# Two transformer blocks on one core: an operand made in another's buffers, weight slabs split a product earlier, the residual input loaded in pieces, and a table spread later on another queue

## The chip, the core and the metric

The program runs on one NeuronCore of a Trainium2 chip. The core has five engines that take their instructions in program order: TensorE (PE) multiplies matrices, VectorE (DVE) and ScalarE (ACT) work elementwise, GpSimd (POOL) does some elementwise work and issues DMAs, and SyncE (SP) only issues DMAs. The engines meet through semaphores. Sixteen DMA engines move the data. The metric is device time of one execution in microseconds, the median of the runs of one kernel.

## The reference, cut to what matters

1,024 tokens of width 1,024 in float32 go through two blocks.

```python
def first_block(x, c, positions, ...):
    ...                       # mod: shift, scale and gate from silu(c) @ w_ada
    h = rms_norm(x, g_pre_mix) * (1.0 + scale1) + shift1
    ...                       # h @ w_in, short convolution and retention
    x = x + gate1 * rms_norm(mix @ w_out, g_post_mix)
    h = rms_norm(x, g_pre_mlp) * (1.0 + scale2) + shift2
    f = square(relu(h @ w_fc1)) @ w_fc2              # 1024 -> 4096 -> 1024
    return x + gate2 * rms_norm(f, g_post_mlp)

def second_block(x, positions, ...):
    z = rmsnorm(x, attn_norm_g) @ w_in
    y_a = dsa_sparse_attention(...)   # top 256 keys a query, bias table rel_bias
    y_b = mla_attention(...)          # latent attention
    x = x + (gate_a * (y_a @ w_branch_a) + gate_b * (y_b @ w_branch_b)) @ w_out
    x = x + square(relu(rmsnorm(x, mlp_norm_g) @ w_ff1)) @ w_ff2
    return rmsnorm(x, final_norm_g)
```

## The kernel before, in words

**Numbers.** Every float32 operand is parted into a rounded high part and the rest, its low part; a product is three matmuls into the same PSUM tile (high by high, high by low, low by high). For a weight slab ACT makes the high part `wh` from the raw slab `wr`, and DVE (in the attention stage POOL) the low part `wl`. Operands that TensorE streams lie in `u` tiles. A half H of the tokens is 512 wide, and activations of a half are eight pieces of 128x512 (256 KB), feature-major.

**Streams.** A `Stream` (`loads_ahead`, `split_ahead`, `next`) holds the order of slabs of one stage. Loads go out on SP in that order as soon as a buffer is promised; an entry can be held until an earlier entry has been split (`after`). SP is strictly in order: a load that waits for a buffer stops all behind it. The background scheduler `bg` steps generators between the products: that is how norms, residuals and stores get their places in the engines' programs.

**MLP of each block.** Both matrix products are done by a seven-product scheme on 2x2 parts. `up_first` makes the product P1 and the part A11 of the hidden layer for sixteen blocks q, two at a time: two half slabs from P1 for each, then two for A11. `up_rest` makes the rest. The hidden layer's four parts lie in HBM (`opd`). `down` runs seven passes P1, P2, P5, P6, P3, P7, P4, each of eight steps d, with a stream `fs` (`down_stream`) for the operands of the passes: A11 and A12 come through a ring of two buffers `t4`, tile name `t`; then the sums S1 = A21 + A22, S2 = S1 + A11 and S4 = S2 + A12 are chained in kept tiles `u` (`kept(d)`), by an SP load and DMAs on POOL's queue that add while they write; then S3 = A11 + A21 for P7 again comes through the ring of two: an SP load of A11, and an adding DMA of A21 on POOL's queue; then A22 for P4 through the ring.

**Residuals.** x of a half is kept in HBM (`xT`). In block 1's output projection the chain `chain_a` squares and adds on POOL (`sq_add`). In the down product `reload` fetches x of a half into a `u` tile with four 512 KB loads on POOL's queue among P7's adding DMAs, `chain_head` and `residual` add the MLP's output to it, and the new x goes back in one store of 2 MB after the norm. In block 2 `before_p7` loads token-major x (`xtokd`) for both halves on SP, 2 MB each; `first_out` and `second_out` add, `finish_last` ends the last half, token block by token block: add, square, reciprocal root, scale, store.

**z phase and attention.** `z_phase` makes the projections of block 2; its last ten products read slabs that POOL loads back (`wh<-slabd`, `wl<-slabd`), two buffers deep. Before them `bias_spread` has POOL write 4 MB (`biasd<-tab`). In `attention` a planner sets the order; SP loads bias slices (`u<-biasd`) and, in between, the last weights of the branches (`wr<-in_w_branch`).

All instructions go through one helper, so the profile gives line 183 for all; they are told apart by tiles.

Of the kernel before, what the change touches and what calls it, by code (L numbers as in the profile page):

```python
# [19 lines left out]
P = 128  # L20
# [323 lines left out]
class Stream:  # L344
# [7 lines left out]
    def __init__(self, m, split=3, slots=None):  # L352
        self.m, self.entries, self.split, self.slots = m, [], split, slots
        self.loads = self.splits = self.done = self.used = self.n_slots = 0
        self.parts, self.given, self.finished = {}, {}, set()
        self.rings = {}
        self.lo_engine = m.nc.vector

# [93 lines left out]
    def loads_ahead(self, n=None):  # L452
        while self.loads < len(self.entries) and (n is None or self.loads < n):
# [34 lines left out]
class Model:  # L488
# [202 lines left out]
    def residual(self, x, f, R, G, acc, engine=None, H=None):  # L691

        nc = self.nc
        for k in range(9):
            if k < 8:
                s = slice(k * T, k * T + T)
                t = self.t2()
                nc.vector.scalar_tensor_tensor(t, f[:, s], G[:, k:k + 1], R, op0=ALU.mult, op1=ALU.mult)
                nc.vector.tensor_add(x[:, s], x[:, s], t)
                if H is not None:  # L700
                    self.store_x(H, x, k)
            if k > 0:
                self.sq_add(acc, x[:, (k - 1) * T:k * T], k == 1, engine)
            yield "vector"
# [509 lines left out]
    def down_stream(self):  # L1214
# [50 lines left out]
        for d in range(8):  # L1265
            ringed(d, "A11", "A21")
# [270 lines left out]
    def block1(self):  # L1537
# [169 lines left out]
        def chain_a(f, acc):  # L1707
            yield from self.chain_head(xs[0], f, acc, G1, None, 0)
# [37 lines left out]
        def before_p7():  # L1746
            xs[0] = self.reload(0, 2)

        def after_p3():
            def chain():  # L1750
                yield from squares(0, 1)
                yield from self.chain_head(xs[0], self.outs[0], acc[0], G2, nc.vector)
# [3 lines left out]
                yield from self.norm_mod(xs[0], self.Rw, g_attn, None, *hs[0])  # L1756
                nc.gpsimd.dma_start(self.xT[:, 0], xs[0])
# [11 lines left out]
        self.down(False, {"P2": after_p2, "P3": after_p3, "P7": after_p7}, {"P7": before_p7, "P4": before_p4})  # L1769
# [9 lines left out]
        xs[0] = None  # L1779
        return xs, hs, self.outs[1], acc[1], G2  # L1780
# [10 lines left out]
    def chain_head(self, x, f, acc, G, engine=None, H=None):  # L1791
# [4 lines left out]
        yield from self.residual(x, f, R, G, acc2, engine, H)  # L1796
        self.Rw = self.r_tile()
# [23 lines left out]
    def bias_spread(self):  # L1821
# [4 lines left out]
        self.nc.gpsimd.dma_start(dst, src)  # L1826
# [446 lines left out]
    def z_phase(self, xs, hs, f, acc, G2):  # L2273
# [10 lines left out]
        def start():  # L2284
            yield from self.chain_head(xs[1], f, acc, G2, nc.vector)
            hs[1] = self.pair()
            yield from self.norm_mod(xs[1], self.Rw, g_attn, None, *hs[1])
            nc.gpsimd.dma_start(self.xT[:, 1], xs[1])
            xs[1] = None
# [59 lines left out]
        self.bias_spread()  # L2349
# [10 lines left out]
        ws.lo_engine = nc.vector  # L2360

# [15 lines left out]
    def attention(self):  # L2377
# [34 lines left out]
        self.branch_weights(starts[15])  # L2412
        self.plan.run()
        ws.lo_engine = self.nc.vector
# [556 lines left out]
    def block2(self):  # L2971
# [3 lines left out]
        xs, hs, xt = [self.reload(0), None], [None, None], [None, None]  # L2975
# [36 lines left out]
        gf = []  # L3012

        def before_p7():
            for H in range(2):
                xt[H] = load(H)

        def load(H):
            x = self.U()
            nc.sync.dma_start(x, self.xtokd[:, H])  # L3020
            return x
# [4 lines left out]
        def first_out():  # L3026
            f, x = self.outs[0], xt[0]
            for b in range(4):
                s = slice(b * D, b * D + D)
                (nc.vector, nc.gpsimd)[b % 2].tensor_add(x[:, s], x[:, s], f[:, s])  # L3030
                yield 2
            for b in range(4):
                s = slice(b * D, b * D + D)
                nc.scalar.activation(f[:, s], x[:, s], AF.Square, accum_out=ss[0][:, b:b + 1])
                yield
            gf.append(f[:, 0:D])
            src = self.a["final_norm_g_2"]
            nc.gpsimd.dma_start(gf[0], bass.AP(tensor=src.tensor, offset=src.offset, ap=[[0, P], [1, D]]))
            self.rsqrt(y[0], ss[0][:, 0:4], 4, 1.0 / D)
            yield 4  # L3040
            for b in range(4):
                s = slice(b * D, b * D + D)
                nc.vector.scalar_tensor_tensor(x[:, s], x[:, s], y[0][:, b:b + 1], gf[0], op0=ALU.mult, op1=ALU.mult)
                yield 1
                nc.sync.dma_start(self.a["out"][b * P:b * P + P], x[:, s])
                yield 1

        def after_p7():
            bg.add(second_out())

        def second_out():
            f, x = self.outs[1], xt[1]
            for b in range(4):
                c0, c1 = (slice(b * D + c * T, b * D + c * T + T) for c in range(2))
                nc.gpsimd.tensor_add(x[:, c1], x[:, c1], f[:, c1])
                nc.vector.tensor_add(x[:, c0], x[:, c0], f[:, c0])
                yield 1
                nc.scalar.activation(f[:, c1], x[:, c1], AF.Square, accum_out=ss[1][:, 2 * b + 1:2 * b + 2])
                yield 1
                nc.gpsimd.tensor_mul(x[:, c1], x[:, c1], gf[0][:, T:D])  # L3060

        self.down(True, {"P3": after_p3, "P7": after_p7}, {"P7": before_p7})
        bg.finish()
        self.finish_last(xt[1], self.last, ss[1], y[1], gf[0])
# [70 lines left out]
```

## Time and profile before

| | before |
|---|---|
| runs, us | 2756.8, 2753.07, 2748.65; median 2753.07 |
| profiled execution, us | 2745.33 |
| its span, us | 2743.6 |
| TensorE busy | 2610.7 us, 95% of the span |
| VectorE, ScalarE, GpSimd busy | 69%, 49%, 14% |
| mean granted TensorE clock | 0.983 of full |
| DMA | 454.86 MB, mean 166 GB/s |

The profiled execution is 1.7 us longer than its span and 7.7 us under the median of the three runs. A timeline row has the start, the duration, the engine (`SPq` is an issue on SP's queue), the operation, what it writes and reads, and in brackets how long the engine stood idle before it and what ended that. `xN` counts merged instructions.

### The profile page before, as it was taken

The page shows a single profiled execution, that of the slowest core. Times are in us where ns is not written, and L with a number is a line of the kernel's source. Part 1 is how long each engine was busy: PE and PEld are TensorE (multiplying, and loading weights), DVE is VectorE, ACT ScalarE, POOL GpSimd, SP SyncE. Part 2 cuts the span into 40 slices and gives each one's busy share as a digit, 9 for nine tenths or more (in the row PEclk, how much of TensorE's full clock was granted, in tenths as well). Part 3 has the DMA queues.
Part 4 walks back from the last instruction along what each step waited for, and adds up shares of the span by engine and source line. Part 5 has one row for each costly group of instructions (what it writes and reads, how often), then busy time and mean ns, then how long its engine had stood idle before and what let it go on. Part 6 is the DMA issues. An engine that isn't in the chain of part 4 may idle for free. (4 is left out here: it accounts for less than half of the span.)

```text
span 2743.6 us, 33563 instructions
## 1 busy us (share of the span) xinstructions
PE 2610.7 (95%) x12037; PEld 2086.5 (76%) x12052; DVE 1881.1 (69%) x3213; ACT 1331.3 (49%) x2192; POOL 391.8 (14%) x409
## 2 busy tenths in 40 slices
PE   5999999899999999999998999899999999999987
PEld 4777777677888888777876777777887788887866
DVE  6684575777665477877889688786567466646657
ACT  4552114465444343445675477784235454433333
POOL 5041111300000020100211411420000000002012
PEclk8999999999999999999999999999999999999999
DMA  6546536654445695845546401453454564459773
GB/s 206 177 139 209 177 119 204 208 192 140 150 133 199 201 271 144 246 110 144 142 147 199 131 14 51 140 167 116 139 170 146 179 238 141 152 188 279 188 207 131
DMA packets 364572, 454.86 MB, mean 166 GB/s; under 512 B 34533, under 2 KB 258708, under 8 KB 363380
## 3 DMA queue, kind: packets, MB, share of 16 engines
q1 hardware_dynamic: 322584, 300.58, 35.1%
q0 software_dynamic: 41488, 151.99, 19.5%
q8 instruction: 95, 1.56, 0.2%
q14 instruction: 73, 0.60, 0.1%
q10 hardware_dynamic: 332, 0.14, 0.0%
HBM read 359.60 MB, written 96.18 MB: 166 GB/s over the span
## 5 line engine op out<-in xcount | busy, mean ns | idle before, releaser
L183 PE MATMUL ps<-u,wh 128*128 128x512 f32 (+1 forms) x3568 | 1138.2, 400 | 27.5 <-DMA wh<-slabd 10.3
L183 PEld LDWEIGHTS ps<-u,wh 128*128 128x128 f32 (+1 forms) x3568 | 668.4, 189 | 196.1 <-ACT wh L183 11.8
L183 PE MATMUL ps<-u,wl 128*128 128x512 f32 (+1 forms) x1784 | 710.3, 398 | 6.7 <-DVE wl L183 6.5
L183 PE MATMUL pd<-u,wh 128*128 128x512 f32 x1600 | 522.8, 408 | 4.7 <-ACT u L183 2.4
L183 PEld LDWEIGHTS ps<-u,wl 128*128 128x128 f32 (+1 forms) x1784 | 336.8, 189 | 95.8 <-DVE wl L183 13.4
L183 PEld LDWEIGHTS pd<-u,wh 128*128 128x128 f32 x1600 | 298.9, 190 | 80.3 <-issue 5.8
L183 DVE TENSOR_TENSOR wl<-wr,wh 128x1024 fp32r<-128x1024 f32 (+3 forms) x209 | 223.8, 1077 | 180.5 <-ACT wh L183 176.8
L183 PE MATMUL pd<-u,wl 128*128 128x512 f32 x800 | 318.1, 398 | 0.0
L183 ACT ACTIVATE wh<-wr 128x1024 fp32r<-128x1024 f32 (+3 forms) x221 | 201.9, 920 | 167.4 <-PE pd L183 74.7
L183 ACT ACTIVATE t<-ps 128x512 f32<-128x512 f32 (+5 forms) x339 | 172.0, 521 | 192.9 <-PE ps L183 182.1
L183 DVE TENSOR_TENSOR t<-ps,t 128x384 fp32r<-128x384 f32 (+3 forms) x354 | 192.4, 563 | 90.6 <-PE ps L183 61.1
L183 ACT ACTIVATE t<-t 128x512 f32<-128x512 f32 (+2 forms) x261 | 163.1, 627 | 160.6 <-DVE t L183 89.1
L183 ACT ACTIVATE u<-t 128x512 fp32r<-128x512 f32 (+4 forms) x174 | 145.3, 839 | 184.9 <-DVE t L183 111.0
L183 DVE TENSOR_TENSOR u<-u 128x512 f32<-128x512 f32 (+3 forms) x144 | 143.3, 999 | 65.6 <-ACT u L183 62.6
L183 ACT ACTIVATE wh<-u 128x1024 fp32r<-128x1024 f32 x96 | 101.3, 1055 | 163.4 <-PE ps L183 117.3
L183 PEld LDWEIGHTS pd<-u,wl 128*128 128x128 f32 x800 | 151.7, 190 | 37.0
L183 DVE TENSOR_TENSOR wl<-u,wh 128x1024 fp32r<-128x1024 f32 x96 | 117.9, 1228 | 87.2 <-ACT wh L183 87.0
L183 PE MATMUL pd<-wh,u 128*128 128x512 f32 x512 | 166.4, 404 | 8.9 <-ACT u L183 7.4
L183 PE MATMUL ps<-wh,u 128*128 128x512 f32 (+1 forms) x576 | 173.7, 383 | 0.6 <-DVE u L183 0.6
L183 DVE TENSOR_TENSOR u<-t,u 128x512 fp32r<-128x512 f32 (+3 forms) x145 | 132.0, 927 | 56.6 <-ACT u L183 56.5
L183 ACT ACTIVATE u<-ps 128x512 f32<-128x512 f32 (+2 forms) x171 | 95.7, 575 | 119.4 <-PE ps L183 113.5
L183 ACT ACTIVATE u<-u,topk 128x768 bf16<-128x768 f32 (+8 forms) x157 | 135.0, 860 | 34.2 <-DVE topk L183 32.3
(193 smaller groups left out, 3407.2 us busy)
## 6 DMA issues: line engine op xcount, KB each, us to landing
wr<-in_w_fc SPq DMA_DIRECT2D x64, 512.0 KB, 4.6
opd<-t SPq DMA_DIRECT2D x128, 256.0 KB, 4.1
t<-opd SPq DMA_DIRECT2D x64, 512.0 KB, 4.4
wr<-in_w_ff SPq DMA_DIRECT2D x64, 512.0 KB, 4.5
wr<-in_w_in SPq DMA_DIRECT2D x56, 512.0 KB, 4.1
u<-opd POOLq DMA_DIRECT2D x48, 512.0 KB, 11.8
u<-in_w_ada POOLq DMA_DIRECT2D x32, 512.0 KB, 4.7
wr<-in_w_out SPq DMA_DIRECT2D x32, 512.0 KB, 3.9
```

What stands on the lines that cost most here:

```text
L183: return fn(*args, **kw)
```

## The change

It does seven things.

1. `up_first` asks for the split of the slabs two entries on after the first of the two A11 products.
2. `down_stream` makes S3 in the kept tiles of S4 (SP load of A21, adding DMA of A11), held until six entries before, instead of in the ring.
3. In block 1's down product and in the z phase x comes in eight pieces of 256 KB on SP into `t2` tiles (eight buffers), and the MLP's output tile takes the sum; xT is stored as four pieces of 512 KB as they are made.
4. `chain_a` adds its squares on DVE, not on POOL.
5. `bias_spread` issues on SP, behind the last slab products.
6. The stream's loads pause while the attention's plan runs.
7. In block 2 the two halves of `xtokd` come in eight pieces each, the first from the end of P3, the second behind the first half's stores in P4; all sixteen adds are on DVE, and the first half's output waits for P7's end.

```diff
@@ up_first
                 self.put_op("A11", q + i, f, 4)
+                if i == 0 and q < 14:
+                    ws.split_ahead(ws.used + 2)
@@ down_stream
-        def chained(d, *ops):
+        def chained(d, *ops, ahead=3):
...
-            s.entry(s.parts_of(lambda: kept(d), D), load, len(s.entries) - 3)
+            s.entry(s.parts_of(lambda: kept(d), D), load, len(s.entries) - ahead)
...
-            ringed(d, "A11", "A21")
+            chained(d, "A21", "A11", ahead=6)
@@ new: x_pieces, residual_in (chain_in calls them)
+        def load(k):
+            if k < 8:
+                xs[k] = self.t2()
+                self.nc.sync.dma_start(xs[k], self.xT[:, H, k * T:k * T + T])
...
+                nc.vector.scalar_tensor_tensor(f[:, s], f[:, s], G[:, k:k + 1], R, op0=ALU.mult, op1=ALU.mult)
+                nc.vector.tensor_add(f[:, s], f[:, s], xs.pop(k))
+                load(k + 2)
+                self.store_x(H, f, k)
+            if k > 0:
+                self.sq_add(acc, f[:, (k - 1) * T:k * T], k == 1, nc.vector)
@@ chain_a
-            yield from self.chain_head(xs[0], f, acc, G1, None, 0)
+            yield from self.chain_head(xs[0], f, acc, G1, nc.vector, 0)
@@ block 1, down product
-        def before_p7():
-            xs[0] = self.reload(0, 2)
...
-                yield from self.chain_head(xs[0], self.outs[0], acc[0], G2, nc.vector)
+                yield from self.chain_in(self.outs[0], acc[0], G2, 0)
...
-                nc.gpsimd.dma_start(self.xT[:, 0], xs[0])
...
-            xs[1] = self.reload(1, 5)
@@ bias_spread, and its place in z_phase
-        self.nc.gpsimd.dma_start(dst, src)
+        self.nc.sync.dma_start(dst, src)
...
-        self.bias_spread()
         for H in range(2):
...
         ws.lo_engine = nc.vector
+        self.bias_spread()
@@ attention
+        ws.loads_ahead()
+        ws.paused = True
         self.plan.run()
+        ws.paused = False
@@ block 2
+        def add_x(H, first):
+            f, xs = self.outs[H], {}
+            order = [(b, c) for c in first for b in range(4)] if H else [(b, c) for b in range(4) for c in first]
+            for n in range(10):
+                if n < 8:
+                    b, c = order[n]
+                    t = xs[n] = self.t2()
+                    nc.sync.dma_start(t, self.xtokd[:, H, b * D + c * T:b * D + c * T + T])
+                    yield 1
+                if n >= 2:
+                    b, c = order[n - 2]
+                    s = slice(b * D + c * T, b * D + c * T + T)
+                    nc.vector.tensor_add(f[:, s], f[:, s], xs.pop(n - 2))
+                    yield 1
+                    if H == 0 or c == 1:
+                        nc.scalar.activation(self.t2(), f[:, s], AF.Square, accum_out=ss[H][:, 2 * b + c:2 * b + c + 1])
```

**Where the order moves.** First ACT in `up_first` of block 1 (`wh<-wr` is the high part of a weight slab, `t<-ps` and the row on the same tile behind it the two passes of the squared relu), one piece of the difference:

```order
+L183 ACTIVATE wh<-wr 128x1024
 L183 ACTIVATE t_4984<-ps 128x512
-L183 ACTIVATE t_5065<-ps 128x512
-L183 ACTIVATE t_5065<-t_5065 128x512
-L183 ACTIVATE wh<-wr 128x1024 x2
-L183 ACTIVATE u<-ps 128x512
-L183 ACTIVATE t_5061<-u 128x512
+L183 ACTIVATE t_5071<-ps 128x512
+L183 ACTIVATE t_5071<-t_5071 128x512
+L183 ACTIVATE wh<-wr 128x1024
```

The two slabs stood in a row behind the second squared relu; now one stands ahead of it and one behind.

Second the end of the z phase, on POOL's queue before:

```order
L183 DMA wh<-slabd 128x1024
L183 DMA wl<-slabd 128x1024
L183 DMA biasd<-tab 8x128x1024
L183 DMA wh<-slabd 128x1024
L183 DMA wl<-slabd 128x1024
```

and on SP's queue in the changed kernel, where `aqd<-t` stores the last latent and `u<-biasd` is the attention's first bias slice:

```order
L183 DMA aqd<-t_12405 128x512
L183 DMA aqd<-t_12441 128x512
L183 DMA biasd<-tab 8x128x1024
L183 DMA wr<-in_w_branch_a 128x4x128
L183 DMA wr<-in_w_branch_b 128x4x128
L183 ISA
L183 DMA u<-biasd 128x896
```

The 4 MB write stood between two slab loads; now nothing of the slabs is behind it.

Third DVE at the end of the program: `wl<-u,wh` and `u<-t,u` are the low parts of P4's last slabs and operands, `u<-ps,u` is the first add of `finish_last`. Before:

```order
L183 TENSOR_TENSOR wl<-u,wh 128x1024
L183 TENSOR_TENSOR u<-t_22241,u 128x1024
L183 TENSOR_TENSOR u<-u 128x512
L183 TENSOR_TENSOR wl<-u,wh 128x1024
L183 TENSOR_TENSOR u<-t_22276,u 128x1024
L183 TENSOR_TENSOR u<-u 128x512
L183 TENSOR_TENSOR u<-t_22312,u 128x1024
L183 TENSOR_TENSOR u<-ps,u 128x512
```

and in the changed kernel:

```order
L183 TENSOR_TENSOR u<-t_22295,u 128x1024
L183 TENSOR_TENSOR u<-t_22329,u 128x1024
L183 TENSOR_TENSOR u<-u,t_22363 128x512
L183 TENSOR_TENSOR u<-u,t_22377 128x512
L183 TENSOR_TENSOR u<-u,t_22393 128x512
L183 TENSOR_TENSOR u<-u,t_22422 128x512
L183 TENSOR_TENSOR u<-u,t_22445 128x512
L183 TENSOR_TENSOR u<-u,t_22450 128x512
L183 TENSOR_TENSOR u<-u,t_22455 128x512
L183 TENSOR_TENSOR u<-u,t_22458 128x512
L183 TENSOR_TENSOR u<-ps,u 128x512
```

The adds of x (`u<-u` before, four of them on POOL besides) stood between P4's low parts; now all eight stand behind the last of them and ahead of `finish_last`.

## Rows read from the trace of the kernel before

**Rows 1.** The page's first part: busy time of the engines.

```profile
PE 2610.7 (95%) x12037; PEld 2086.5 (76%) x12052; DVE 1881.1 (69%) x3213; ACT 1331.3 (49%) x2192; POOL 391.8 (14%) x409
```

**Rows 2.** Windows, block 1: busy us (count) of PE, PEld, DVE, ACT, POOL; clock.

```profile
500.00:560.00 60.00, 49.75 (x198) 37.48 (x197) 50.60 (x79) 34.10 (x53) 20.19 (x19) 0.91 0.57 175
560.00:640.00 80.00, 72.06 (x304) 55.02 (x303) 63.39 (x98) 53.08 (x86) 2.19 (x4) 1.00 0.58 190
```

**Rows 3.** Windows of four of the stretches whose granted clock is 0.50.

```profile
525.90:532.70 6.80, 5.23 (x14) 3.94 (x15) 6.42 (x17) 1.71 (x3) 2.25 (x2) 0.50 0.84 252
...
1112.90:1119.70 6.80, 6.13 (x16) 4.88 (x17) 6.42 (x17) 1.55 (x3) 0.00 (x0) 0.50 1.02 325
...
1491.80:1502.00 10.20, 4.87 (x11) 3.38 (x12) 9.58 (x37) 0.00 (x0) 0.00 (x0) 0.50 0.62 232
...
2638.70:2645.50 6.80, 6.45 (x14) 4.63 (x15) 4.63 (x4) 1.21 (x2) 1.54 (x3) 0.50 0.89 299
```

**Rows 4.** Waits of PE: releaser, us in total, times, longest.

```profile
PE ps L183 <- ACT wh L183: 10.0, 9, 2.0
...
PE ps L183 <- DVE wl L183: 6.5, 14, 0.5
```

**Rows 5.** Timeline of block 1's `up_first`, PE: one of eight places.

```profile
594.44 0.74 PE L183 MATMUL ps<-u,wh 128*128 128x512 f32 x2 [1.19 <-ACT wh L183]
595.70 0.50 PE L183 MATMUL ps<-u,wl 128*128 128x512 f32 x1 [0.52 <-DVE wl L183]
```

**Rows 6.** Timeline around `chain_a` in block 1's output projection.

```profile
525.70 1.71 POOL L183 TENSOR_TENSOR t<-t,t 128x512 f32<-128x512 f32 x1 [1.22 <-ACT t L183]
...
527.47 1.11 PE L183 MATMUL ps<-ident,t 128*128 128x128 f32 x4 [4.91 <-POOL t L183]
...
538.20 0.51 PE L183 MATMUL ps<-u,wh 128*128 128x512 f32 x1 [3.06 <-ACT u L183]
```

**Rows 7.** Timeline of P7 in block 1.

```profile
1103.82 0.85 POOL L183 DMA_DIRECT2D t<-opd  x1 [7.81 <-DMA t<-opd]
...
1112.31 0.50 PE L183 MATMUL pd<-u,wh 128*128 128x512 f32 x1 [2.26 <-ACT u L183]
```

**Rows 8.** Timeline of P4 in block 1, PE.

```profile
1181.44 1.12 PE L183 MATMUL pd<-ident,tiny 128*128 128x128 f32 x4 [4.80 <-DVE tiny L183]
```

**Rows 9.** Timeline of the last slab products of the z phase.

```profile
1475.62 0.55 POOL L183 DMA_DIRECT2D wh<-slabd  x1 [9.03 <-PE pd L183]
...
1497.05 1.22 PE L183 MATMUL ps<-u,wh 128*128 128x512 f32 x2 [10.30 <-DMA wh<-slabd]
```

**Rows 10.** DMA issues: count, KB each, us to landing (the last: from 1476 to 1477.3 us).

```profile
opd<-t SPq DMA_DIRECT2D x128, 256.0 KB, 4.1
...
biasd<-tab POOLq DMA_DIRECT2D x1, 4096.0 KB, 30.3
...
u<-xtokd SPq DMA_DIRECT2D x2, 2048.0 KB, 17.0
...
gates<-t SPq DMA_DIRECT2D x1, 512.0 KB, 7.1
```

**Rows 11.** Timeline of the attention stage: low part on POOL, load on SP, PE.

```profile
1757.63 2.40 POOL L183 TENSOR_TENSOR wl<-wr,wh 128x1024 fp32r<-128x1024 f32 x1
...
1760.06 0.39 SPq L183 DMA_DIRECT2D wr<-in_w_branch_a  x1
...
1767.59 1.22 PE L183 MATMUL pd<-u 128*128 128x512 f32 x2 [4.61 <-DVE topk L183]
```

**Rows 12.** Timeline of P7 in block 2.

```profile
2639.02 0.80 PE L183 MATMUL pd<-wh,u 128*128 128x512 f32 x1 [4.42 <-ACT u L183]
...
2650.79 0.50 PE L183 MATMUL pd<-wh,u 128*128 128x512 f32 x1 [2.74 <-ACT u L183]
```

**Rows 13.** Timeline of the end, DVE.

```profile
2718.10 1.23 DVE L183 TENSOR_TENSOR u<-t,u 128x1024 fp32r<-128x1024 f32 x1 [1.30 <-ACT u L183]
2720.62 0.69 DVE L183 TENSOR_TENSOR u<-ps,u 128x512 f32<-128x512 f32 x1 [1.29 <-PE ps L183]
```

More of the change, by code (lines that the diff above doesn't have):

```diff
@@ L357, in __init__ @@
         self.lo_engine = m.nc.vector
+        self.paused = False
     def entry(self, steps, load=None, after=0, half=None):
@@ L452, in loads_ahead @@
     def loads_ahead(self, n=None):
-        while self.loads < len(self.entries) and (n is None or self.loads < n):
+        while not self.paused and self.loads < len(self.entries) and (n is None or self.loads < n):
             e = self.entries[self.loads]
@@ L703, in residual, with x_pieces, residual_in @@
                 self.sq_add(acc, x[:, (k - 1) * T:k * T], k == 1, engine)
+            yield "vector"
+    def x_pieces(self, H):
+        xs = {}
+        def load(k):
+            if k < 8:
+                xs[k] = self.t2()
+                self.nc.sync.dma_start(xs[k], self.xT[:, H, k * T:k * T + T])
+        return load, xs
+    def residual_in(self, f, R, G, acc, load, xs, H):
+        nc = self.nc
+        for k in range(9):
+            if k < 8:
+                s = slice(k * T, k * T + T)
+                nc.vector.scalar_tensor_tensor(f[:, s], f[:, s], G[:, k:k + 1], R, op0=ALU.mult, op1=ALU.mult)
[4 more added lines that the diff above has]
+                self.sq_add(acc, f[:, (k - 1) * T:k * T], k == 1, nc.vector)
             yield "vector"
@@ L1796, in chain_head, with chain_in @@
         yield from self.residual(x, f, R, G, acc2, engine, H)
+        self.Rw = self.r_tile()
+        yield from self.rstd_bcast(acc2, D, self.Rw)
+        yield
+    def chain_in(self, f, acc, G, H):
+        load, xs = self.x_pieces(H)
+        R = self.r_tile()
+        yield from self.rstd_bcast(acc, D, R)
+        acc2 = self.acc_tile()
+        load(0)
+        load(1)
+        yield from self.residual_in(f, R, G, acc2, load, xs, H)
         self.Rw = self.r_tile()
@@ L2284, in start @@
         def start():
-            yield from self.chain_head(xs[1], f, acc, G2, nc.vector)
+            yield from self.chain_in(f, acc, G2, 1)
             hs[1] = self.pair()
-            yield from self.norm_mod(xs[1], self.Rw, g_attn, None, *hs[1])
-            nc.gpsimd.dma_start(self.xT[:, 1], xs[1])
-            xs[1] = None
+            yield from self.norm_mod(f, self.Rw, g_attn, None, *hs[1])
         g0 = bg.add(start())
@@ L2974, in block2 @@
         self.ya = self.yb = None
-        xs, hs, xt = [self.reload(0), None], [None, None], [None, None]
+        xs, hs = [self.reload(0), None], [None, None]
         acc = self.out2(xs[0], merged[0], 0)
@@ L3011, in block2 @@
         ss, y = [self.tiny(8), self.tiny(8)], [self.tiny(4), self.tiny(4)]
[L3012 to L3021, printed above, removed]
+        gf, p7 = [], []
+        def add_x(H, first):
[14 more added lines that the diff above has]
+                        nc.scalar.activation(self.t2(), f[:, s], AF.Square, accum_out=ss[H][:, 2 * b + c:2 * b + c + 1])
         def after_p3():
@@ L3026, in first_out @@
         def first_out():
-            f, x = self.outs[0], xt[0]
+            f = self.outs[0]
+            yield from add_x(0, (0, 1))
+            v = ss[0].rearrange("p (b c) -> p b c", c=2)
+            nc.vector.tensor_add(y[0], v[:, :, 0], v[:, :, 1])
+            self.rsqrt(y[0], y[0], 4, 1.0 / D)
+            while not p7:
+                yield
             for b in range(4):
                 s = slice(b * D, b * D + D)
-                (nc.vector, nc.gpsimd)[b % 2].tensor_add(x[:, s], x[:, s], f[:, s])
-                yield 2
@@ L3032, in first_out, with after_p7 @@
[L3032 to L3036, printed above, removed]
+                nc.vector.scalar_tensor_tensor(f[:, s], f[:, s], y[0][:, b:b + 1], gf[0], op0=ALU.mult, op1=ALU.mult)
+                yield 1
+                nc.sync.dma_start(self.a["out"][b * P:b * P + P], f[:, s])
+                yield 1
+        def after_p7():
+            gf.append(self.U()[:, 0:D])
@@ L3037, in first_out @@
             src = self.a["final_norm_g_2"]
             nc.gpsimd.dma_start(gf[0], bass.AP(tensor=src.tensor, offset=src.offset, ap=[[0, P], [1, D]]))
[L3039 to L3046, printed above, removed]
@@ L3048, in after_p7 @@
-        def after_p7():
+            p7.append(1)
             bg.add(second_out())
         def second_out():
-            f, x = self.outs[1], xt[1]
+            f = self.outs[1]
+            yield from add_x(1, (1, 0))
             for b in range(4):
[L3054 to L3060, printed above, removed]
@@ L3062, in block2 @@
-        self.down(True, {"P3": after_p3, "P7": after_p7}, {"P7": before_p7})
+                s = slice(b * D + T, b * D + D)
+                nc.gpsimd.tensor_mul(f[:, s], f[:, s], gf[0][:, T:D])
+        self.down(True, {"P3": after_p3, "P7": after_p7}, {})
         bg.finish()
-        self.finish_last(xt[1], self.last, ss[1], y[1], gf[0])
+        self.finish_last(self.outs[1], self.last, ss[1], y[1], gf[0])
     def finish_last(self, x, acc, ss, y, gf):
```

9 lines of the change are left out of this document (4 added, 5 removed).

## The prediction

> **What bounds the kernel now.** The page's first part comes first: TensorE is busy for 95% of the span, VectorE for 69%, ScalarE for 49% [rows 1]. So no other engine is full over the whole, and a change that leaves the matmuls alone can win only where TensorE stands still or runs slowly. The windows by stage come next, to find those places and to see who is full there: around block 1's output projection and first up product TensorE works 49.75 of 60 us and 72.06 of 80, and VectorE 50.60 and 63.39 in the same stretches, so VectorE is near its limit just where I hope for time [rows 2]. Then the stretches with granted clock 0.50, the lower of the two levels (1.2 of 2.4 GHz): each lies at or behind a stop of TensorE of some microseconds, and in it the matmuls take twice as long [rows 3]. I price this at half of TensorE's busy time there: 5.23 gives 2.6 us, 6.13 gives 3.1, 4.87 gives 2.4, 6.45 gives 3.2. Last the timelines at the stops, to see what ended each [rows 5 to 9, 11, 12]. A stop is worth its length plus that half.
>
> **The sum, part by part.** Each edit aims at stops that can be named.
>
> *Up product, slabs a product earlier.* ScalarE makes two high parts in a row behind the squared relu, VectorE the low parts behind them, and TensorE waits for both [rows 5]. There are eight such places, four in each block. The waits for ScalarE sum to 10.0 us in nine, and without the longest, 2.0, which is at the program's start, 8.0 in eight; the waits for VectorE are 0.5 each, 4.2 in eight [rows 4]. Together 12.2. The slab that moves ahead costs no work, only order. What could keep part of it is VectorE: 63.39 us of work in the 72.6 that would be left of block 1's stretch [rows 2]. Ends 6 and 12; I take 11, near the upper end, because the wait was ended by ScalarE's order, and ScalarE has 53 us of work in those 80.
>
> *chain_a's adds on VectorE.* TensorE waits 4.91 us for POOL's last add of 1.71, and 3.06 us ten microseconds on, and loses 2.6 to the clock: 10.6 [rows 3, 6]. Seven adds move; a VectorE add of this size takes 0.69 [rows 13], so VectorE gets 4.8 us of work in a stretch where it has 9.4 free [rows 2]. The chain is as long as VectorE needs for everything before it in its program, so the stop need not go with POOL. Ends 0 and 10.6; I take 5.
>
> *S3 in the kept tiles, block 1.* In P7 the adding DMA for a ring buffer is issued at 1103.82, behind a wait of 7.81 us for its SP load, and TensorE then stands 2.26 us [rows 7] and works 6.13 us at half clock [rows 3]: 5.4. After the change these loads wait only for P3 to split the tile six steps earlier, and no reload of x lies between them on POOL's queue. What is late next would be the weights on SP. Ends 2 and 5.4; I take 5.
>
> *P4 in block 1.* A stop of 4.80 us on the small transposes of the norm, which stand behind an operand's low part in VectorE's program [rows 8]; that operand came late beside the 2 MB store of x. The store is now made in 512 KB pieces before. Ends 0 and 4.8; I take 4.
>
> *Table behind the last slabs.* POOL issues a slab load at 1475.62 behind the 4 MB write, which takes 30.3 us to land, and TensorE waits 10.30 us for that slab [rows 9, 10]; with 2.4 for the clock 12.7. On SP and behind the slabs, nothing of the z phase waits for it; its first reader is a bias slice behind the whole first part of the attention. A store that SP issued while the write was running landed in 7.1 us, while the slab on POOL's own queue took over 20 [rows 9, 10], so small loads on POOL at the start of the attention lose some 3 us each at worst, and several have that much slack. The Trainium skill says in "DMA: Bandwidth & Descriptors", section "Queues, rings and completion order", that each DMA engine goes round between the queues it has work for, packet by packet; the two landings agree with it, and by it the table cannot hold back another queue for its whole length. Ends 6 and 12.7; I take 11.5.
>
> *Loads paused in the attention.* SP stands at a branch weight until POOL has made the low part of an earlier one (2.40 us, done at 1760.03); the bias slices behind it come late and TensorE waits 4.61 us [rows 11]. With the pause these loads leave the plan. They are issued again when the branches begin, beside the gates' loads; the branches' first slabs are there already, so I cost this at nothing, and at 4 us if those slabs are not. Ends 0 and 4.6; I take 4.5.
>
> *Block 2's x in pieces, S3 there.* The two 2 MB loads ahead of P7 take 17.0 us to land [rows 10], P7's operands come late beside them, and TensorE stands 4.42 and 2.74 us [rows 12], with 3.2 for the clock [rows 3]: 10.4. The loads are now small and lie elsewhere, and P7's operands are six steps ahead. Ends 5 and 10.4; I take 10.
>
> *The end, a loss.* The second half's eight adds stand behind P4's last low part, which ends at 2719.33, and ahead of `finish_last`'s first add, which began at 2720.62 [rows 13]. Eight adds of 0.69 are 5.5 us, so that add could begin at 2724.9 at the earliest, 4.3 later. But the last three of the eight loads find no free `t2` buffer: they wait for the first adds and squares of the same half. The sixth can be issued at about 2720.1 and lands 4.1 us later by the row of 256 KB stores [rows 10], the eighth about 1.5 behind it; then come the last adds, and `finish_last` begins at some 2726.7. The four token blocks behind it run one after the other as before, so the whole loss arrives at the end. Ends 4 and 9; I take 6. The Trainium skill ("DMA: Bandwidth & Descriptors", "Anatomy of one DMA — SWDGE (gpsimd) path") gives a fit of 2.0 us plus the bytes at 436 GB/s, an estimate of 2.6 us for such a piece; with it the loss would be some 4.5 in place of 6.
>
> Sum: 11 + 5 + 5 + 4 + 11.5 + 4.5 + 10 = 51, less 6, is **45 us**. The profiled execution, 2745.3 us (1.7 more than its span), would become 2700; it lies 7.7 under the median of the runs, 2753.07, so on the scale of the runs I forecast **2708**.
>
> **Rivals.**
>
> *Part of the stops move to VectorE (22%).* VectorE has 114 of 140 us of work in the two windows of [rows 2] and gets 4.8 more, and TensorE alone needs 122 there. If the order of VectorE's program, not POOL or ScalarE, is what holds the chain, the up product and `chain_a` give 8 in place of 16; if P4's transposes and P7 are caught by VectorE's new adds of x too, those two give half, 4.5 less; and if the table's write slows the attention's first loads, 5 less. That is 45 - 17.5 = 27.5, a time of 2726. For it speaks how full VectorE is; against it that most of the named waits ended with a DMA or ScalarE.
>
> *SP's pieces hold back the weights: slower (6%).* 32 loads of x go out on SP in order, most of them behind a wait for a `t2` buffer that a VectorE add frees, and behind them lie weight slabs and operands of P7, P4 and the z phase. If SP stands there longer than the slabs already in hand last, TensorE stops as it does now for a late slab, 10.30 us plus 2.4 for the clock [rows 3, 9]. Five such stops, one in each half's chain and one more, are 63.5 us, and the time is 2708 + 63.5 = 2771. It decides from the fourth or fifth stop on, when the loss passes 45. A row that speaks for it is SP held by one branch weight at 1760.06 and a stop of 4.61 us behind [rows 11]; against it stands that only two pieces are asked for ahead of the adds, with eight buffers, and that the operands have left the ring. The Trainium skill's rule "Batch DMAs to ≥1 MiB for ≥75% of peak" (same page, section "Bandwidth") speaks for this rival. In this trace eight pieces one after the other would be 33 us at 4.1 each, against 17.0 for 2 MB [rows 10], but nothing on the path waits for the eight until the end.
>
> *The operands stay late: no change (6%).* S3's adding DMAs still come behind something on POOL's queue, the table's cost reappears in the attention, and only the up product's 11 remain, less the 6 at the end: 2748.
>
> **How the numbers follow.** The forecast, most stops gone, has 66%, with its own range of 2690 to 2722: all upper ends give 60.7 less 4, 2696, and some shorter half-clock stretches and waits of half a microsecond beside the same stops, which I left out of the sum, a few more. The first rival reaches to about 2744, where all lower ends would be (19 less 9, 10 us). The range 2690 to 2736 holds nearly all of the forecast and most of that rival. A measurement of this kernel tells about 0.3%, 8 us, from no change. Faster by more than that is 66 and 22, 88%; the same 6%; slower 6%.
>
> **What would show it.** Right: no wait of over a microsecond for `wh` in either `up_first`; `wh<-slabd` landing in about 5 us at the end of the z phase and no stop there; P7 of both blocks without a wait for operands, and no half clock in it; the attention's bias slices not behind `wr<-in_w_branch`; the first add of `finish_last` some 7 us, not 1.3, behind the last low part of P4. Wrong: new waits of SP for `t2` buffers with late `wr` slabs behind them, a stop at the transposes of `chain_a` ended by VectorE, or a new wait for DMA at the start of the attention. A time over 2736 would mean that stops have moved, not gone; one under 2690 that I priced the clock too low.

## The result, and the profile after

The changed kernel takes 2705.04 us (median of 4 runs, 2704.01 to 2708.1), the kernel before 2750.86 (4 runs); the ratio is 0.9832, 95% interval 0.9813 to 0.9852. That is 45.8 us less, where 45 were forecast. The profiled execution has a span of 2702.0 us, 41.6 less than before. The page's first part now reads (before: [rows 1]):

```profile
PE 2594.4 (96%) x12037; PEld 2082.5 (77%) x12052; DVE 1887.3 (70%) x3231; ACT 1332.3 (49%) x2200; POOL 366.2 (14%) x393
```

The total hides where it came from. The two traces have the same matmuls in nearly the same order, so the start of one and the same matmul can be compared. In the table each line is how much the distance after minus before grew since the line above; the first line, ahead of every edit, shows how far two executions differ without one.

| up to (us before, after) | what lies in it | forecast | measured |
|---|---|---|---|
| 500.17, 501.67 | not touched | 0 | +1.5 |
| 660.02, 658.36 | chain_a, block 1's up product | -5 and about -6.5 | -3.2 |
| 1150.06, 1142.72 | block 1's down product, P7 in it | -5 | -5.7 |
| 1190.16, 1181.63 | its P4 | -4 | -1.2 |
| 1540.03, 1518.63 | z phase with the last slabs | -11.5 | -12.9 |
| 1700.29, 1681.25 | attention, first part | 0 | +2.4 |
| 1800.02, 1775.16 | attention, bias slices | -4.5 | -5.8 |
| 2200.00, 2166.44 | block 2's up product | about -4.5 | -8.7 |
| 2700.01, 2650.51 | block 2's down product | -10 | -15.9 |
| 2743.6, 2702.0 | the end | +6 | +7.9 |

The lines sum to -41.6. The rows behind them follow. Waits of TensorE after, against [rows 4]: the waits for low parts of slabs (`wl`) fall from 14 with 6.5 us to 2 with 0.5, and of nine for high parts one is left, the 2 us at the program's start. The waits for ScalarE's `u` grew; they were 7.5 us in 5.

```profile
PE ps L183 <- ACT u L183: 10.6, 6, 4.1
...
PE ps L183 <- ACT wh L183: 2.0, 1, 2.0
```

The timeline of TensorE after, from `chain_a` to the start of `up_rest` in block 1, where [rows 5, 6] stood before:

```profile
530.72 0.88 PE L183 MATMUL ps<-ident,t 128*128 128x128 f32 x4 [2.72 <-DVE t L183]
...
534.65 1.09 PE L183 MATMUL ps<-ident,tiny 128*128 128x128 f32 x4 [3.05 <-DVE tiny L183]
...
537.97 0.79 PE L183 MATMUL ps<-u,wh 128*128 128x512 f32 x1 [2.23 <-ACT u L183]
...
640.45 0.79 PE L183 MATMUL ps<-u,wh 128*128 128x512 f32 x1 [4.14 <-ACT u L183]
...
643.65 0.79 PE L183 MATMUL ps<-u,wh 128*128 128x512 f32 x1 [2.41 <-DVE u L183]
```

The stop ended by POOL is gone from `chain_a`, but 2.72, 3.05 and 2.23 us stand where 4.91 and 3.06 stood; two of them are ended by VectorE at the transposes, which the prediction named as a sign of being wrong. And behind `up_first`, whose own waits are gone, there is a new stop of 4.14 and 2.41 us, on the operands of the second half (`u`), which the chain on VectorE and ScalarE makes. At these two places 13.7 and 6.8 us lie at half clock; before it was 6.8 and 3.4, both around `chain_a`:

```profile
531.00:544.70 13.70, 7.98 (x22) 4.93 (x21) 11.42 (x27) 5.53 (x8) 0.54 (x1) 0.50 0.27 79
640.20:647.00 6.80, 4.14 (x9) 2.96 (x10) 6.70 (x12) 3.64 (x7) 0.00 (x0) 0.50 0.00 0
```

In block 1's down product (before: [rows 7, 8]) the first row is TensorE in P7, where a short wait for an operand is left, the last two what P4's operand and transposes wait for:

```profile
1121.81 0.51 PE L183 MATMUL pd<-u,wh 128*128 128x512 f32 x1 [1.53 <-ACT u L183]
...
1167.76 1.06 ACT L183 ACTIVATE u<-t 128x1024 fp32r<-128x1024 f32 x1 [4.04 <-DMA t<-opd]
...
1172.91 0.90 PE L183 MATMUL pd<-ident,tiny 128*128 128x128 f32 x3 [4.01 <-DVE tiny L183]
```

At the end of the z phase there is no stop ([rows 9] before): TensorE is busy for 80.98 of 81 us, and VectorE, nearly full itself, for 75.22. In block 2's P3 to P4 ([rows 12] before) it stands nowhere. The windows after:

```profile
1460.00:1541.00 81.00, 80.98 (x371) 65.88 (x371) 75.22 (x160) 34.85 (x64) 25.32 (x25) 1.00 0.65 205
...
2566.00:2616.00 50.00, 50.00 (x216) 40.23 (x216) 34.83 (x33) 19.33 (x22) 4.82 (x6) 1.00 0.95 282
2616.00:2650.50 34.50, 34.50 (x149) 27.79 (x148) 27.00 (x42) 15.85 (x24) 0.00 (x0) 1.00 0.22 69
```

The end after, VectorE ([rows 13] before): eight adds in a row between the last low part and `finish_last`'s first add, which begins 9.1 us behind that low part's end (2669.83) in place of 1.3. VectorE has no idle time in between. SP issues the last three loads of x at 2670.46, and they land in 2.7 us, ahead of the adds that need them. But POOL multiplies beside the adds, and four of the eight take 1.78 us each (the last row is one of them); the first adds took some 0.6.

```profile
2668.61 1.22 DVE L183 TENSOR_TENSOR u<-t,u 128x1024 fp32r<-128x1024 f32 x1 [3.01 <-ACT u L183]
2669.75 9.29 DVE L183 TENSOR_TENSOR u<-u,t 128x512 f32<-128x512 f32 x8
...
2678.97 0.68 DVE L183 TENSOR_TENSOR u<-ps,u 128x512 f32<-128x512 f32 x1
```

```profile
2670.46 1.55 SPq L183 DMA_DIRECT2D t<-xtokd  x3
2671.28 6.62 POOL L183 TENSOR_TENSOR u<-u 128x512 f32<-128x512 f32 x4 [73.15 <-ACT t L183]
2671.56 1.78 DVE L183 TENSOR_TENSOR u<-u,t 128x512 f32<-128x512 f32 x1
```

### The profile page after: what moved, and what is told of

It reads as the page before. It is cut to its first block, busy times and chain, and to the rows that moved or that the text cites. A ratio compares the mean times of both kernels' runs of the same rounds, so it can differ in the third digit from the quotient of the medians.

```text
span 2702.0 us, 33618 instructions
## 1 busy us (share of the span) xinstructions
PE 2594.4 (96%) x12037; PEld 2082.5 (77%) x12052; DVE 1887.3 (70%) x3231; ACT 1332.3 (49%) x2200; POOL 366.2 (14%) x393
## 4 chain that ended last, share of the span: by engine, by line
PE 76%; DVE 9%; issue 5%; ACT 4%; DMA 3%; POOL 1%; SPq 0%; POOLq 0%; DVEq 0%; ACTq 0%
PE ps L183 51%; PE pd L183 25%; DVE u L183 4%; ACT u L183 3%; DVE t L183 3%; ACT t L183 1%; DMA t<-in_w_in 1%; DVE tiny L183 1%; DMA slabd<-t 1%; DVE wl L183 1%; DVE topk L183 1%; POOL u L183 1%; ACT wh L183 0%; DMA t<-opd 0%; DMA u<-opd 0%
## 5 line engine op out<-in xcount | busy, mean ns | idle before, releaser
L183 DVE TENSOR_TENSOR u<-u 128x1024 fp32r<-128x1024 f32 (+3 forms) x154 | 153.2, 998 | 64.7 <-ACT u L183 59.1
L183 ACT ACTIVATE u<-t 128x512 fp32r<-128x512 f32 (+4 forms) x158 | 128.3, 816 | 131.9 <-DVE t L183 100.9
L183 POOL DMA_DIRECT2D u<-opd x64 | 55.2, 1020 | 868.8 <-DMA wr<-in_w_fc 370.8
L183 ACT ACTIVATE u<-u 128x1024 fp32r<-128x1024 f32 (+8 forms) x111 | 97.4, 889 | 121.2 <-issue 57.1
```

What stands on the lines that cost most here:

```text
L183: return fn(*args, **kw)
```

## Experiments

All start from the changed kernel. Times of one run are the profiled execution's, to be set beside the changed kernel's own, 2704.01 us. At 500 us, ahead of every edit, TensorE's place in these runs already differs from the changed kernel's by -1.6 to +0.9 us, so gains and losses at a place are given as growth from there on, and a difference of 2 us between totals of single runs shows nothing.

**Block 1's up product: is it the slabs' order?** The early split is taken out in block 1 alone.

```diff
-                if i == 0 and q < 14:
+                if i == 0 and q < 14 and self.late:      # set at the start of block 2
```

> The changed kernel without the early slab split in block 1's up product; block 2 keeps it. Theory of the chain: block 1's up product is held by the second half's residual and norm chain on VectorE, whose last quarter ends at about 645 us in either kernel; the eight waits for slabs (7.4 us) come back in block 1, but the two stops at the start of the rest of the up product (4.14 and 2.41 us, with 6.8 us at half clock) go. TensorE's place at the first products of the rest of the up product then differs by less than 2 us from the changed kernel's, and the time is 2703 to 2708. Theory of the slabs: the early split removed 7.4 us and the stop behind it has a cause of its own; then it stays, TensorE arrives there 7 us later, and the time is 2710 to 2714.

Measured: 2705.89 us, one run. The four pairs of waits are back (1.19 us at 594.83 and so on), the stop at 640 us is gone; TensorE is 2.0 us later than in the changed kernel at 660 us, where 0.9 of that stood at 500 us. So in block 1 this edit moved a wait of some 9 us to another place and won 1 to 2.

**Can the chain be brought forward?** The scheduler's lead of VectorE over its model of TensorE is 1.5 us; in both up products it is set to 5.

```diff
+        self.clock.LEAD = 5.0       # at the start of up_first, back to 1.5 behind it
```

> The changed kernel; in both up products the background scheduler may run VectorE's chain 5 us ahead of its model of TensorE in place of 1.5, so the second half's chain stands earlier between the low parts. Nothing is added or left out. Theory of the order: VectorE had some 12 us idle between 587 and 624 us, waiting for high parts with the chain behind them in its program; then the stops at the start of the rest of the up product (4.14 and 2.41 us, and half clock) shrink to under 2 us without new stops of over 3 us in all, and the time is 2695 to 2700. Theory of the capacity: VectorE is full there, the chain ahead makes the slabs' low parts late, TensorE waits for those instead, and the time is 2703 to 2708.

Measured: 2718.59 us (4 runs, 2716.63 to 2720.31). Neither theory holds as put. The stop at 640 us is gone; but TensorE now waits inside the up products, and not for low parts alone: the waits for ScalarE's `u` are 14 with 16.7 us (6 with 10.6 in the changed kernel). ScalarE's evacuations of PSUM (`u<-ps`) stand behind chain steps that wait for VectorE. From TensorE, block 1, then ScalarE ahead of the second of these stops:

```profile
588.02 0.74 PE L183 MATMUL ps<-u,wh 128*128 128x512 f32 x2 [1.03 <-ACT u L183]
592.19 0.72 PE L183 MATMUL ps<-u,wh 128*128 128x512 f32 x2 [1.10 <-ACT u L183]
...
605.91 0.74 PE L183 MATMUL ps<-u,wh 128*128 128x512 f32 x2 [1.00 <-ACT u L183]
```

```profile
591.02 0.63 ACT L183 ACTIVATE u<-t 128x512 fp32r<-128x512 f32 x1 [0.70 <-DVE t L183]
591.55 0.58 ACT L183 ACTIVATE u<-ps 128x512 f32<-128x512 f32 x1
```

Block 2, which had no stop to cure, lost some 8 us of the 13. A smaller lead, in block 1 only, was tried later:

```diff
+        self.clock.LEAD = 2.5       # around block 1's up_first
```

> The changed kernel with the chain allowed 2.5 us ahead in place of 1.5, in block 1's up product only (5 us, in both blocks, made the chain end in time and TensorE wait for ScalarE instead). If some place between gives both, the stop of 4.14 and 2.41 us at the start of the rest of the up product shrinks by more than the up product loses, TensorE is there 3 us or more earlier, and the time is 2699 to 2703. If the chain's length on VectorE and ScalarE, from block 1's output projection to the rest of the up product, is what counts, TensorE is there within 2 us of the changed kernel and the time is 2703 to 2708.

Measured: 2704.01 us, one run. The stop shrinks to 2.66 and 0.97 us, and the up product loses most of that: from 500 to 660 us TensorE gains 0.3 us. The chain's length, over two engines that wait for each other in program order, is what counts, as the second theory had it.

**Was it POOL that held chain_a?**

```diff
-            yield from self.chain_head(xs[0], f, acc, G1, nc.vector, 0)
+            yield from self.chain_head(xs[0], f, acc, G1, None, 0)
```

> The changed kernel with the first half's adds of squares in block 1 back on POOL. Theory that VectorE holds the chain: TensorE's stops between 520 and 550 us (8.4 us in the changed kernel) turn back into one ended by POOL with nearly the same sum, TensorE is at the start of the rest of the up product within 2 us of the changed kernel, and the time is 2703 to 2708. Theory that POOL's adds held it, as forecast: 5 us or more come back and the time is 2709 to 2714.

Measured: 2708.98 us, one run. The total lies just over the first range, but the place decides: POOL's stop of 5.03 us is back at 527.31, of the others one of 3.06 and one of 0.65 are left, and from 500 to 660 us TensorE loses 0.3 us. What is longer lies in the attention's first part (+2.7 us at 1560, with 10.2 us at half clock there), far from the edit. Edit 4 was worth nothing measurable in this place.

**The table: queue or place?** Two more cases beside before (POOL, early) and the change (SP, late).

```diff
+        self.bias_spread()          # on SP, ahead of the last ten slab products
         for H in range(2):
...
         ws.lo_engine = nc.vector
-        self.bias_spread()
```

> The changed kernel with the 4 MB table write still on SP's queue, but at its old place ahead of the last ten slab products. Theory of the queue: the slabs came late because they stood behind the write on POOL's own queue; on SP the write can run beside them, no stop of over 2 us comes back there, the small stops and the 3.4 us at half clock at the start of the attention (2.4 us) go, and the time is 2702 to 2706. Theory of the bytes: the write takes the DMA engines from the slabs wherever it is issued, or holds SP's stores and with them the buffers; then TensorE stands 5 to 10 us in the last slab products and the time is 2709 to 2717.

Measured: 2703.24 us, one run; TensorE busy for 81.00 of 81.00 us over the last slabs, and the half-clock stretch at 1551 us is gone; TensorE gains 2.4 us from 1540 to 1600. The other case, POOL's queue at the late place:

```diff
-        self.nc.sync.dma_start(dst, src)
+        self.nc.gpsimd.dma_start(dst, src)
```

> The changed kernel with the table write back on POOL's queue, but at its new place behind the last slab products. With the run that had it on SP at the old place this makes four cases of queue and place. Theory of the queue: what POOL issues behind it, the small loads at the start of the attention, lands some 15 to 25 us late, as the slabs did; TensorE stands at least 8 us there and the time is 2712 to 2722. Theory of the place: late is enough whatever the queue, and the time is 2703 to 2707.

Measured: 2717.02 us, one run. The two small loads that POOL issues behind the write take 12.6 us to land; before they took 2.3, in the changed kernel 5.2. DMA issues of the three kernels (before from 1557 us, changed from 1536, this one from 1537), then ScalarE, which waits for such a load, and TensorE in this run, with 17.1 us at half clock around it:

```profile
t<-u POOLq DMA_DIRECT2D x2, 128.0 KB, 2.3
```

```profile
t<-u POOLq DMA_DIRECT2D x2, 128.0 KB, 5.2
```

```profile
t<-u POOLq DMA_DIRECT2D x2, 128.0 KB, 12.6
```

```profile
1551.71 1.05 ACT L183 ACTIVATE u<-t 32x1024 fp32r<-32x1024 f32 x1 [10.46 <-DMA t<-u]
...
1552.81 1.22 PE L183 MATMUL pd<-u 96*128 96x512 f32 x2 [6.36 <-ACT u L183]
```

The time is that of the first theory, though the loads are less late than it said and the stop is shorter (6.36 us, not 8). With four cases the queue is shown: on POOL's queue the write makes what stands behind it late, 21 us for the slab before and 12.6 here; on SP the place is worth some 2 us.

**P7: the ring or the bytes?**

```diff
-            chained(d, "A21", "A11", ahead=6)
+            ringed(d, "A11", "A21")
```

> The changed kernel with S3 back in the ring of two t4 buffers (SP load of A11, adding DMA of A21 on POOL's queue); x still comes in pieces. Theory of the ring: P7's stops came from the two buffers, since a load can start only when an operand two steps earlier is split; they come back in both blocks, some 5 us in block 1 and 8 to 12 in block 2 with the clock, and the time is 2715 to 2722. Rival, the bytes: they came from the x loads that shared queue and DMA engines with the operands (2 MB twice, 17 us, in block 2; reloads on POOL's queue in block 1), which are gone; then P7 stands still for less than 3 us in all and the time is 2703 to 2708.

Measured: 2725.43 us, one run, 20 over the changed kernel and 3 over the upper end of the first theory; of that block 1's P7 brings 9.1 us and block 2's 10.6. P7 stops again in both blocks, though x comes in pieces:

```profile
1129.27 0.80 PE L183 MATMUL pd<-u,wh 128*128 128x512 f32 x1 [4.02 <-ACT u L183]
...
2618.37 0.50 PE L183 MATMUL pd<-wh,u 128*128 128x512 f32 x1 [1.22 <-ACT u L183]
...
2635.30 0.80 PE L183 MATMUL pd<-wh,u 128*128 128x512 f32 x1 [3.12 <-ACT u L183]
```

So the ring of two is enough to stop P7, and S3's new place is worth more than any other edit undone here. Whether the old 2 MB loads would stop P7 without the ring was not run, nor were the loads in pieces (points 3 and 7 of the change) undone by themselves.

**The pause in the attention.**

```diff
-        ws.paused = True
+        ws.paused = False
```

> The changed kernel without the pause of the weight loads during the attention's plan. If the pause is what removed the stop of 4.61 us, it returns near 1748 us with SP standing at a branch weight ahead of bias slices, with some 2 us of half clock, and the time is 2709 to 2713. Rival: the stop hung on the table write or on where POOL stood; then no stop of over 2.5 us comes back and the time is 2703 to 2706.

Measured: 2709.22 us, one run, with the stop back where it was expected, 3.29 us at 1748.52, and 5.5 us lost around it.

**The end.** First the second half's adds all in P4, stepped beside the first half's output.

```diff
-                    yield 1                      # in add_x, twice
+                    yield 1 - H                  # a step every tick for the second half
...
-            bg.add(second_out())
+            bg.add(second_out(), lane=1)
```

> The changed kernel, with the second half's eight loads and adds of x stepped beside the first half's output, so that seven of eight adds and all loads lie inside P4 (on VectorE between the low parts). Theory of the place: the end is 7.9 us longer than before only because the adds stand behind P4's last low part and the last loads wait for their buffers; then finish_last's first add comes 1 to 2 us behind the last low part and the time is 2696 to 2699. Rival, the queue: SP's x loads wait for t2 buffers and hold P4's operands behind them; TensorE then stops in P4 and the time is 2703 or more.

Measured: 2702.63 us (4 runs, 2701.73 to 2704.23). Both theories hold in part: the end is 7.9 us shorter; but P4 has new stops, with 3.4 us at half clock behind each of the two longer, and loses 7.4 us, so by the trace next to nothing is won. The later is an add that waits for its load of x, with P4's last low part queued behind it (VectorE, then TensorE); ahead of the earlier a low part took 2.30 us beside POOL (last section):

```profile
2669.69 0.69 DVE L183 TENSOR_TENSOR u<-u,t 128x512 f32<-128x512 f32 x1 [2.32 <-DMA t<-xtokd]
```

```profile
2651.57 0.73 PE L183 MATMUL ps<-wh,u 128*128 128x512 f32 x2 [1.80 <-DVE u L183]
...
2672.71 0.50 PE L183 MATMUL ps<-wh,u 128*128 128x512 f32 x1 [1.83 <-DVE u L183]
```

Next, four adds spread over P4, one behind it, three inside `finish_last` in VectorE's waits for ScalarE; the table on SP early.

```diff
+            for b in range(4):
+                s = add(b)                   # the columns whose squares are taken early
...
             nc.scalar.activation(junk[:, s], x[:, s], AF.Square, accum_out=ss[:, 2 * b:2 * b + 1])
+            if b < 3:
+                left[b + 1]()                # the next token block's other add
```

> The changed kernel with the table write on SP at the old place, and the end rearranged: the second half's loads of x start with P4, four of its adds (those whose squares are taken early) lie one to a step in P4, one behind the last low part, and three inside finish_last, where VectorE waits for ScalarE. If the losses were places in VectorE's program and late x loads, no stop of over 1 us comes up in P4, finish_last begins 1 to 2 us behind the last low part, and with some 2 us at the start of the attention the time is 2694 to 2698. Rival: any add in P4 makes a low part late, as in the run that had all eight there; then TensorE stops again in P4 and the time is 2700 to 2704.

Measured: 2700.93 us (5 runs, 2696.5 to 2711.15), in the rival's range. One stop is left, 1.55 and 0.94 us at 2652.58, behind an add that waits 0.77 us for its load. So the first add was put later, and, which the expectation does not name, the next ones one step apart in place of two:

```diff
-            yield 1
+            yield 5                          # between the first three loads and the first add
...
-                yield 2
+                yield 1                          # from one add to the next
```

> The run with spread adds, with the first add in P4 one step later, so that its load of x has landed; the rest as there (table write on SP at the old place). If the stop of 1.55 and 0.94 us in P4 there came only from VectorE waiting 0.77 us for that load, it goes with its 3.4 us at half clock, and the time is 2696 to 2700, 5 to 9 below the changed kernel. Rival: the adds themselves make the low parts late; then the stop moves to a later step and the time is 2700 to 2704.

Measured: 2698.48 us (5 runs, 2696.02 to 2706.8), ratio to before 0.982, interval 0.9799 to 0.9841. The stop is gone, in the time that was expected (which of the two lines did it is not shown), and this is the fastest version found, 6.6 us under the changed kernel by the medians (5.6 by the profiled spans); the two intervals overlap, so the gain over the changed kernel is small against the scatter.

Last, in that version, the stop in block 1's P4: the rotary tables' loads go behind P4's operands.

```diff
-        nc.gpsimd.dma_start(self.rope[:, 0:D], ...)
+        nc.sync.dma_start(self.rope[:, 0:D], ...)     # the second load alike
```

> The run with adds one step later in P4, and the two loads of the rotary tables issued by SP behind the last operand loads of P4, in place of POOL's queue, where they started at 1154 us and ran beside P4's operands. If these loads are what makes the operand of P4 in block 1 late (issued at 1161, used at 1168, a stop of 4 us on the transposes), the stop falls below 2 us, its 3.4 us at half clock may go, and the time is 2692 to 2696. Rival: the operand is late because the ring of two lets it start only after an earlier operand is split; then the stop stays at 3.5 us or more and the time is 2696 to 2700.

Measured: 2700.33 us (5 runs, 2697.51 to 2707.63), not the time expected, though the place did what the first theory said: no stop at the transposes, and against the run before TensorE gains 6.0 us in P4 and 2.2 more by the middle of the z phase. All of it is given back from 1528 us on. POOL and VectorE ahead of that stop, TensorE, and then the same two VectorE rows in the run before:

```profile
1521.09 8.61 POOL L183 TENSOR_TENSOR u<-u 32x1024 fp32r<-32x1024 f32 x3 [3.76 <-issue]
...
1521.42 2.77 DVE L183 SCALAR_TENSOR_TENSOR u<-u,topk,t 128x512 bf16<-128x512 f32 x1
1524.11 3.36 DVE L183 TENSOR_TENSOR wl<-wr,wh 128x1024 fp32r<-128x1024 f32 x1
```

```profile
1527.39 0.68 DVE L183 SCALAR_TENSOR_TENSOR t<-ps,u 128x512 f32<-128x512 f32 x1
...
1528.12 1.22 PE L183 MATMUL ps<-u,wh 128*128 128x512 f32 x2 [4.28 <-DVE t L183]
```

```profile
1526.45 0.75 DVE L183 SCALAR_TENSOR_TENSOR u<-u,topk,t 128x512 bf16<-128x512 f32 x1
1527.12 1.22 DVE L183 TENSOR_TENSOR wl<-wr,wh 128x1024 fp32r<-128x1024 f32 x1
```

TensorE waits for VectorE to read a PSUM tile (`t<-ps,u`), which stands in its program behind the selection of keys and a low part. VectorE works there without a pause, so TensorE can be earlier only as far as VectorE is. Two of VectorE's instructions took 2.77 and 3.36 us beside POOL in place of 0.75 and 1.22: that is 4.2 of the stop's 4.28 us. So by these rows most of the stop hangs on where POOL's work falls; no run moved that work to show it.

## Why the prediction was right, and where its terms were not

The time, the sign and the range held. The terms did not: block 1's up product with `chain_a` came out 8 us under its forecast, P4 in block 1, the attention's start and the end together 7 under, block 2's up product and down product together 10 over. That these cancelled to within a few us is luck. The mechanism held for P7, the table, the attention and block 2's up product.

- *Up product and chain_a in block 1: the steps that failed.* "I take 11, near the upper end, because the wait was ended by ScalarE's order": in block 1 mostly the place changed, and `chain_a`'s adds on VectorE, priced at 5, brought nothing that can be measured. The first two experiments show the second half's chain as the bound. The first rival named the effect, VectorE in block 1, and priced the two terms, of both blocks, at 8 in place of 16; measured were 3.2 in block 1 and 8.7 in block 2. In block 2, whose chain lacks the residual, the stops went and stayed away: the four places brought 7.0, not 4.5, and three waits for low parts at the start of `up_rest`, which the sum left out, 1.7. Part of that is how a stop is read: before the wait at 594.44 the last matmul began at 592.85 and the next could have followed 0.23 us later, so the stop was 1.36 us and the row's bracket says 1.19; with waits of 0.5 us such shares count.
- *P7: right mechanism, too small in block 2.* The forecast took the waits from the x loads and the ring together; the experiment shows that the ring alone, with x in pieces, makes about 20 us in the two blocks. In block 2 the sum had two stops and one half-clock stretch; waits of half a microsecond behind them and a second stretch (3.4 us at 2652.4) were left out.
- *P4 in block 1: the step that failed* is "that operand came late beside the 2 MB store of x". The store is small now and the operand as late; the last experiment shows that in the changed kernel it is the rotary tables' loads, which the change only starts earlier (1153.8 us, before 1162.4). How much the 2 MB store did beside them before stays open.
- *The table: right.* 12.9 us for 11.5, and the small loads pay some 3 us (5.2 against 2.3), as said; that cost 2.4 us with a half-clock stretch, where the forecast had nothing.
- *The attention: right*, 5.8 for 4.5, and no new wait for the branch weights.
- *The end: right place, another cause for the size*, 7.9 for 6. From the low part's end to `finish_last`'s add there are 9.1 us, where the forecast had 7.4 (2726.7 less 2719.33). It took the late loads for the limit; they landed in 2.7 us, not 4.1, and no add waited for one. What it left out is POOL: four multiplies ran beside the adds, and four adds took 1.78 us in place of the forecast's 0.69, 4.4 us in all.
- *The rival on the slower side* did not come: no stop of the changed kernel is ended by a weight slab that SP held back.
- *Two slips in the arithmetic* change nothing: the upper ends as stated add to 60.5, not 60.7, and the time with all lower ends is 2743, not 2744.

## What to carry to other kernels

Before a stop is counted as won, look for the chain that was hidden behind it: the work that must end at the next boundary shows whether TensorE can arrive there earlier at all. A ring of two for an operand that needs two transfers, one after the other, was a wait built in here; a dead tile as a buffer, asked for six steps ahead, removed it. Put a large write on the queue on which nothing urgent stands behind it, and put what remains for the last half into the waits of the final chain, not in front of it. Look at what POOL does beside VectorE where VectorE is on the path.

## What the runs showed of the hardware that was not expected

VectorE slows beside POOL's elementwise work, for which the forecast had no price. It shows in three places: at the end of the changed kernel (adds of 1.78 us), in the last experiment (2.77 and 3.36 us), and in the run with all adds in P4, where a low part took 2.30 us while POOL multiplied beside it; its neighbour of the same shape took 1.22:

```profile
2648.09 1.22 DVE L183 TENSOR_TENSOR wl<-u,wh 128x1024 fp32r<-128x1024 f32 x1
2649.07 1.36 POOL L183 TENSOR_TENSOR u<-u 128x512 f32<-128x512 f32 x1 [52.56 <-ACT t L183]
2649.22 2.30 DVE L183 TENSOR_TENSOR u<-t,u 128x1024 fp32r<-128x1024 f32 x1
```

The Trainium skill ("SBUF — State Buffer", section "SBUF: two separate sides") says that a VectorE operation with two SBUF inputs and a GpSimd operation that reads SBUF need one shared pair of ports: whichever starts first has it for its whole instruction, and the other waits. The 1.08 us that were lost here agree with that, being most of POOL's 1.36.
